# Halved first loads, an earlier weight split and 256-column Fourier products in a token-mixing kernel

## The chip, the cores and the metric

The kernel runs on one core of a Trainium2 chip. The time is the device time of one execution in microseconds; the median of three runs is 1002.89 us (1002.65 to 1003.63). The engines are named as in the profile: PE multiplies matrices, PEld loads its weights, DVE and ACT are the vector and the scalar engine, POOL is little used here, and SP issues the DMAs.

## What is computed

One layer of a diffusion backbone over 1024 latent tokens and 256 context tokens of width 1024, in float32. Cut to what matters:

```python
x = x + sincos_2d(n_lat, D)                              # position
h = rms_norm(x, norm_g) * (1 + sc) + sh                  # sc, sh, gt from silu(c) @ ada_w + ada_b
u_lru, z_lru, u_fft, z_fft, u_pool, z_pool, gates = split(h @ w_in)   # 56 blocks of 128 columns
ya = (bidirectional RG-LRU(conv(u_lru)) * silu(z_lru)) @ proj_a
yb = (fourier_mix(u_fft) * silu(z_fft)) @ proj_b         # fft2 over tokens and channels, 4 groups of 128
yc = (pool_mix(u_pool) * silu(z_pool)) @ proj_c
m = sigmoid(g0) * ya + sigmoid(g1) * yb + sigmoid(g2) * yc
out = rms_norm(x + gt * (m @ w_out)) * final_g
```

## The kernel before

Everything lies transposed, channels on the 128 partitions and tokens along the free axis. A float32 product is made of three products of float32r parts: each operand is split into a high part (ACT casts it) and a low part (DVE subtracts it), and high x low, low x high and high x high are added up in PSUM. So each weight and each activation costs a cast on ACT and a subtraction on DVE before PE can use it.

**The first 120 us** are written out in program order for all engines. The eight `z` blocks of 128 output columns (the gate of the LRU branch) are computed first, and the first six of them before the norm is known: `xs` is x times the weights' scale `gsc`, without the norm's factor `rstd` (`xs_hi`, `xs_lo`, L337 to L342), and `rstd` is multiplied in afterwards. `wave(k, ...)` (L355) does the products of one 128-channel slice k for a set of blocks: three terms, each over the blocks and both 512-token halves, 24 products of 512 columns for the four blocks z0 to z3 (`FIRST`). Their weights come in four chunks of two k each (`load_chunk`, L273), z4 to z7 as whole blocks. For each k DVE does a dot product of `ada` and `silu(c)` for `gsc` (`dot_scale`), adds the position (`add_pos`), makes the low part of xs and adds up the squares (`squares_add`, L422). Before the waves PE runs sixteen dummy products (`warm_up(16)`, L398), each of which the profile shows as two records.

Wave 7 goes block by block: z2, z0, z1, then the sum over the partitions of the squares (`ss`, a product with ones), then z3; ACT copies z2, z0 and z1 out (`copy_out`, L403) and computes `rstd` by Ln and Exp (`rstd_part`). Then blocks z4 and z5 (`NEXT`) run over all k. In the order of ACT the split of z5's weights (L473) stands behind the norm and behind the third `copy_out`. Blocks z6 and z7 (`LAST`) use the normed `ht`, which DVE and ACT make meanwhile.

**The rest** is a list of units (L1111 to L1114) in which PE's order is fixed: 46 more blocks of `w_in` with the LRU's work between them, pooling (`m`), the projections `c` (pooling) and `b` (Fourier) of 24 products each, and the Fourier steps S1 (`s`) and S2 (`t`) in the order `c0 c1 s0 c2 s1 t0 c3 s2 t1 c4 s3 t2 c5 t3`. There the order of the other engines and the buffers of the pools come from a planner that simulates the program; buffers are `p4` (36 of 4 KB a partition), `p2`, and `pacc` (four PSUM tiles of two banks).

S1 of a group (L931) multiplies the folded tokens, nine blocks of 128 (eight and one extra for the middle row), by the channel transform of the group: cosine for blocks 0 to 3 and the extra one, sine for 4 to 7. Each block takes three products of 128 columns. `group_dft` (L906) makes those transforms, high and low, in four separate p2 tiles. The result is split again for S2. `load_fold` (L921) fetches and splits the tokens of a group beforehand.

Of the kernel before, what the change touches and what calls it, by code (L numbers as in the profile page):

```python
# [15 lines left out]
NK = 8  # L16
HALF = 512
# [11 lines left out]
def tile_hybrid_mixer(  # L29
# [106 lines left out]
    class Weight:  # L136
        def __init__(self, name, src, shape=(128, NK, 128), pools=(praw, pwt, pwt)):
            self.name, self.shape, self.pools = name, shape, pools
            self.raw = f4(name + "_f", shape, pools[0])
            SP.dma_start(out=self.raw, in_=src)  # L140

        def mk(self):
            self.hi, self.lo = (r4(self.name + n, self.shape, p) for n, p in zip(("_h", "_l"), self.pools[1:]))
# [98 lines left out]
    with tc.manual_schedule(engines={ET.PE}):  # L242
# [22 lines left out]
        def load_ada(n):  # L265
            ada_t[n] = f4(f"ada{n}")
            SP.dma_start(out=ada_t[n], in_=ada[n])
# [11 lines left out]
        def load_w(nm):  # L279
            wt[nm] = Weight("w" + nm, item(nm)[1], KK, (praw, p4, p4))  # L280

        SP.dma_start(out=sb[0], in_=cc[0:1, :].to_broadcast([128, 1024]))
        load_ada(8)
        for k in range(NK):
            SP.dma_start(out=xt[k], in_=xT[k])
            if k == 0:
                SP.dma_start(out=pos, in_=k_pos)
                SP.dma_start(out=sml, in_=small)
            else:
                load_ada(8 + k)  # L290
            if k in (0, 2, 4):
                load_chunk(k // 2)
        SP.dma_start(out=edge, in_=k_edge)

# [59 lines left out]

        def wave(k, ws, src):  # L355
            for n in range(3):
                for nm, hi, lo in ws:
                    o = pacc_t[nm]
                    for h in range(2):
                        x = src[k][n == 2][:, H[h]]  # L360
                        PE.matmul(out=bank(o, h), lhsT=lo if n == 1 else hi, rhs=x,  # L361
                                  start=k == 0 and n == 0, stop=k == NK - 1 and n == 2)

        def chunk(k, names):
            w = chunks[k // 2]
# [29 lines left out]

        act(sb[0], sb[0], AF.Silu)
        V.tensor_scalar(b1, sml[:, O_AB + 8:O_AB + 16], 1.0, 0.0, op0=ALU.add, op1=ALU.add)
        warm_up(16)  # L398
        sqs, zv = None, {}
        pacc_t = {"z0": acc("z0"), "z1": acc("z1"), "z2": acc("z2"), "z3": acc("z3")}  # L400

# [23 lines left out]
                del sq[k]  # L425


        add_pos(0)
        for k in range(NK):
            dot_scale(k, 0)  # L430
            if k == 0:
                chunks[0].ready()
            xs_hi(k)
            sq[k] = f4(f"sq{k}")
            act(sq[k], xt[k], AF.Square)
            if k < NK - 1:
                add_pos(k + 1)
            if k:
                squares_add(k - 1)
            xs_lo(k)  # L440
            if k % 2 and k < NK - 1:
                chunks[k // 2 + 1].ready()
            if k == 0:
                load_chunk(3)
            if k == 3:
                load_w("z4")
            if k == 4:
                load_w("z5")
            if 1 < k < 6:
                load_ada(k - 2)  # L450
            if k < NK - 1:
                wave(k, chunk(k, FIRST), xs)
        act(rss[:, 0:1], eps, AF.Ln)
        wt["z4"].ready()
        wave(7, chunk(7, ["z2"]), xs)
        copy_out("z2")
        wave(7, chunk(7, ["z0"]), xs)
        wave(7, chunk(7, ["z1"]), xs)
        ps = acc("ss")
        ps = [ps[:, sl] for sl in H]  # L460
        squares_add(7)
        for h in range(2):
            PE.matmul(out=ps[h], lhsT=ones, rhs=sq[0][:, H[h]], start=True, stop=True)
        sq.clear()
        copy_out("z0")
        rstd_part([rstd[:, H[0]], rstd[:, H[1]]], ps)
        copy_out("z1")
        wave(7, chunk(7, ["z3"]), xs)
        dot_shift(0, 0)
        load_ada(4)  # L470
        dot_shift(1, 0)
        load_ada(5)
        wt["z5"].ready()  # L473
        dot_shift(2, 0)
        load_ada(6)
        dot_shift(3, 0)
# [429 lines left out]

        def group_dft():
            cg, fw = pq["cg"], pq["fw"]
            pq["h"], pq["l"] = [], []
            ps = acc("pq")  # L910
            for n in range(2):
                PE.matmul(out=ps[:, H[n]], lhsT=cg[:, n * 128:(n + 1) * 128], rhs=fw, start=True, stop=True)
            for n in range(2):
                hi, lo = r2(f"pqh{n}"), r2(f"pql{n}")
                split(hi, lo, ps[:, H[n]])
                pq["h"].append(hi)
                pq["l"].append(lo)

        ff = {}

# [9 lines left out]

        def S1(g):  # L931
            fh, fl, ex = ff.pop(("f", g))
            o, o2 = acc(f"s1_{g}"), acc(f"s1e_{g}")
            for b in range(8):
                n = b // 4
                ph, pl = pq["h"][n][:, g * 128:(g + 1) * 128], pq["l"][n][:, g * 128:(g + 1) * 128]
                sl = slice(b * 128, (b + 1) * 128)
                mm3(o[:, sl], [(fh[:, sl], fl[:, sl], ph, pl)])
            mm3(o2[:, 0:128], [(ex[:, 0, :], ex[:, 1, :], pq["h"][0][:, g * 128:(g + 1) * 128],
                                pq["l"][0][:, g * 128:(g + 1) * 128])])  # L940
            ah, al = r4(f"ah{g}"), r4(f"al{g}")
            split(ah, al, o)
            xe = p1.tile([128, 2, 128], F32R, tag="t1", name=f"xe{g}")
            split(xe[:, 0, :], xe[:, 1, :], o2[:, 0:128])
            ff["a", g] = (ah, al, xe)

        ysb, ysc = [None] * 4, [None] * 4
# [436 lines left out]
```

## Time and profile before

| | |
|---|---|
| median of 3 runs | 1002.89 us (1002.65 to 1003.63) |
| the profiled execution | 1002.09 us, of which its span (first to last instruction) 1000.3 us |
| PE busy | 988.7 us (99%), 4686 products |
| weight loads (PEld) | 810.3 us (81%) |
| DVE, ACT, POOL busy | 582.1 (58%), 522.2 (52%), 21.7 us (2%) |
| DMA | 152.53 MB, 43% of 16 engines |
| mean granted clock of PE | 0.997 |

Each line of a timeline has the start and the length of an instruction, or of several alike (x8), in microseconds, then engine, line, operation and `output<-inputs`; in brackets the idle time of the engine before it and what ended it. Successive products overlap in the array, so the distance between two starts is what a product costs, not its length. The chain that ended last is 94% PE, 4% ACT and 1% DMA.

### The profile page before, as it was taken

To read this page: it belongs to the slowest core of one execution; us is meant where nothing else is said; L and a number is where in the kernel's file an instruction comes from. 1 tells how busy PE (TensorE), PEld (TensorE's weight loads), DVE (VectorE), ACT (ScalarE), POOL (GpSimd) and SP (SyncE) were. 2 spreads that over 40 slices of the span, in tenths; PEclk is the share of its full clock that TensorE was granted. 3 is DMA by queue.
4 is the path that set the end of the run, shared out by engine and by line. 5 is a ranking of instruction groups with operands and counts; after the bars stand their busy time and mean duration, and the time that the engine had idled before them with its cause. 6 is when DMAs were issued, how large, how long until landed. Compare 5 with 4: busy or idle time off the path is not lost.

```text
span 1000.3 us, 11785 instructions
## 1 busy us (share of the span) xinstructions
PE 988.7 (99%) x4686; PEld 810.3 (81%) x4686; DVE 582.1 (58%) x746; ACT 522.2 (52%) x618; POOL 21.7 (2%) x22
## 2 busy tenths in 40 slices
PE   9989999999999999999999999999999999999997
PEld 5868788878788887888878888778888888888886
DVE  6959457538557485563845628256565674456063
ACT  4443464295793956939599394884332221213131
POOL 0000000000000000000000000000000000000341
PEclk9999999999999999999999999999999999999999
DMA  9532595131322222343243312357655785324272
GB/s 347 229 108 83 197 382 231 64 105 67 108 103 96 101 85 90 127 166 134 70 167 105 132 64 95 106 184 258 217 185 187 244 315 188 137 91 134 71 252 75
DMA packets 48838, 152.53 MB, mean 152 GB/s; under 512 B 6544, under 2 KB 10128, under 8 KB 48784
## 3 DMA queue, kind: packets, MB, share of 16 engines
q1 hardware_dynamic: 48640, 151.53, 43.0%
q8 instruction: 37, 0.61, 0.2%
q10 hardware_dynamic: 144, 0.26, 0.1%
q14 instruction: 17, 0.14, 0.0%
HBM read 114.01 MB, written 37.75 MB: 152 GB/s over the span
## 4 chain that ended last, share of the span: by engine, by line
PE 94%; ACT 4%; DMA 1%; DVE 0%; issue 0%; POOL 0%; DVEq 0%; SPq 0%; POOLq 0%
PE z L361 9%; PE pi L193 3%; PE pg L193 3%; PE o L195 3%; PE pi L195 3%; PE o L193 3%; PE o L194 3%; PE pi L194 3%; PE pg L194 3%; PE ppa L195 3%; PE ppa L193 3%; PE pu L195 3%; PE pg L195 3%; PE pu L194 3%; PE pu L193 3%; PE ppa L194 3%
## 5 line engine op out<-in xcount | busy, mean ns | idle before, releaser
L114 ACT ACT_TABLE_LOAD x74 | 94.9, 1283 | 2.0 <-PEq L1374 0.7
L117 DVE TENSOR_TENSOR i<-i,xc 128x1024 f32<-128x1024 f32 x16 | 19.0, 1223 | 58.9 <-ACT i L114 58.9
L194 PE MATMUL o<-wo_l,mh 128*128 128x512 f32 (+1 forms) x136 | 51.2, 377 | 0.0
L195 PE MATMUL o<-wo_h,mh 128*128 128x512 f32 (+1 forms) x136 | 51.2, 376 | 0.0
L193 PE MATMUL o<-wo_h,ml 128*128 128x512 f32 (+1 forms) x136 | 51.2, 376 | 0.0
L193 PE MATMUL pi<-hh,i_l 128*128 128x512 f32 x128 | 50.8, 397 | 0.0
L193 PE MATMUL ph<-hh,h_l 128*128 128x512 f32 x128 | 50.5, 395 | 0.2
L193 PE MATMUL pg<-hh,g_l 128*128 128x512 f32 x128 | 50.5, 394 | 0.0
L194 PE MATMUL pi<-hl,i_h 128*128 128x512 f32 x128 | 49.9, 390 | 0.0
L195 PE MATMUL ph<-hh,h_h 128*128 128x512 f32 x128 | 49.9, 390 | 0.0
L195 PE MATMUL pi<-hh,i_h 128*128 128x512 f32 x128 | 49.9, 390 | 0.0
L194 PE MATMUL ph<-hl,h_h 128*128 128x512 f32 x128 | 49.8, 389 | 0.0
L194 PE MATMUL pg<-hl,g_h 128*128 128x512 f32 x128 | 49.8, 389 | 0.0
L195 PE MATMUL pg<-hh,g_h 128*128 128x512 f32 x128 | 49.8, 389 | 0.0
L193 PE MATMUL pu<-hh,u_l 128*128 128x512 f32 x128 | 49.8, 389 | 0.0
L194 PE MATMUL pu<-hl,u_h 128*128 128x512 f32 x128 | 49.8, 389 | 0.0
L195 PE MATMUL pu<-hh,u_h 128*128 128x512 f32 x128 | 49.8, 389 | 0.0
L193 PE MATMUL ppa<-yh,pa_l 128*128 128x512 f32 x128 | 49.8, 389 | 0.0
L194 PE MATMUL ppa<-yl,pa_h 128*128 128x512 f32 x128 | 49.8, 389 | 0.0
L195 PE MATMUL ppa<-yh,pa_h 128*128 128x512 f32 x128 | 49.8, 389 | 0.0
L129 ACT CAST xh<-xc 128x1024 fp32r<-128x1024 f32 x8 | 8.4, 1054 | 75.1 <-DVE xc L120 52.8
L120 DVE SCALAR_TENSOR_TENSOR junk<-ada,sb 128x1024 bf16<-128x1024 f32 x32 | 39.0, 1219 | 13.5 <-DMA ada<-in_ada 13.5
(378 smaller groups left out, 2614.8 us busy)
## 6 DMA issues: line engine op xcount, KB each, us to landing
ada<-in_ada SPq DMA_DIRECT2D x32, 512.0 KB, 8.6
x<-in_xT SPq DMA_DIRECT2D x8, 512.0 KB, 10.0
u_f<-in_w_in SPq DMA_DIRECT2D x8, 512.0 KB, 4.0
i_f<-in_w_in SPq DMA_DIRECT2D x8, 512.0 KB, 4.5
k_i<-ei SPq DMA_DIRECT2D x8, 512.0 KB, 2.9
z<-k_z SPq DMA_DIRECT2D x8, 512.0 KB, 5.4
k_y<-z SPq DMA_DIRECT2D x8, 512.0 KB, 2.6
h_f<-in_w_in SPq DMA_DIRECT2D x8, 512.0 KB, 4.3
```

Source lines behind the costliest of these rows:

```text
L114: S.activation(out=o, in_=i, func=func, **kw)
L117: V.tensor_tensor(o, a, b, op=op)
L120: V.scalar_tensor_tensor(o, a, s, b, op0=op0, op1=op1, **kw)
L129: S.copy(hi, src)
L193: PE.matmul(out=o, lhsT=wl, rhs=xh, start=first and i == 0, stop=False)
L194: PE.matmul(out=o, lhsT=wh, rhs=xl, start=False, stop=False)
L195: PE.matmul(out=o, lhsT=wh, rhs=xh, start=False, stop=last and i == n - 1)
L361: PE.matmul(out=bank(o, h), lhsT=lo if n == 1 else hi, rhs=x, start=k == 0 and n == 0, stop=k == NK - 1 and n == 2)
```

## The change

- **First loads.** `small` goes ahead of `ada8` and x0. x0 and the first weight chunk come in two halves each (x by tokens, weights by k); for the other k, `ada` is loaded ahead of x. `first_block` does the first two k's weights and the first x: ACT casts the weights of k = 0, then the two halves of x as DVE adds their positions, then the weights of k = 1; DVE makes the low parts. In wave 0 the first term runs over the first token half of all four blocks before the second half.
- **Dummies.** Seven instead of sixteen.
- **Norm.** `squares_add(7)` is issued ahead of wave 7, `copy_out("z0")`, two shift dots and the split of z5's weights ahead of the wave of z1, `copy_out("z1")` ahead of the sum of squares.
- **Fourier step.** High and low transform lie beside each other in one p4 tile, so that the high part of a token block is multiplied by both in one product of 256 columns, which go to two column ranges of PSUM; the low part is multiplied by the high transform (128 columns). This holds for seven of the eight blocks; block 7 and the extra one keep three products of 128 columns. ACT copies one column range to SBUF (`v`) and DVE adds the other; the split for S2 reads `v`. PSUM tiles stay two a group.

```diff
@@ -137,7 +137,8 @@
         def __init__(self, name, src, shape=(128, NK, 128), pools=(praw, pwt, pwt)):
             self.name, self.shape, self.pools = name, shape, pools
             self.raw = f4(name + "_f", shape, pools[0])
-            SP.dma_start(out=self.raw, in_=src)
+            if src is not None:
+                SP.dma_start(out=self.raw, in_=src)
 
         def mk(self):
             self.hi, self.lo = (r4(self.name + n, self.shape, p) for n, p in zip(("_h", "_l"), self.pools[1:]))
@@ -279,16 +280,21 @@
         def load_w(nm):
             wt[nm] = Weight("w" + nm, item(nm)[1], KK, (praw, p4, p4))
 
+
         SP.dma_start(out=sb[0], in_=cc[0:1, :].to_broadcast([128, 1024]))
+        SP.dma_start(out=sml, in_=small)
         load_ada(8)
-        for k in range(NK):
+        SP.dma_start(out=pos, in_=k_pos)
+        w0 = Weight("wc0", None, (128, 4, 2, 128), CHUNK_POOLS[0])
+        for h in range(2):
+            SP.dma_start(out=xt[0][:, H[h]], in_=xT[0][:, H[h]])
+            SP.dma_start(out=w0.raw[:, :, h, :],
+                         in_=w_in[B_ZLRU:B_ZLRU + 4, :, h, :].rearrange("b p o -> p b o"))
+        chunks.append(w0)
+        for k in range(1, NK):
+            load_ada(8 + k)
             SP.dma_start(out=xt[k], in_=xT[k])
-            if k == 0:
-                SP.dma_start(out=pos, in_=k_pos)
-                SP.dma_start(out=sml, in_=small)
-            else:
-                load_ada(8 + k)
-            if k in (0, 2, 4):
+            if k in (2, 4):
                 load_chunk(k // 2)
         SP.dma_start(out=edge, in_=k_edge)
 
@@ -354,12 +360,13 @@
 
         def wave(k, ws, src):
             for n in range(3):
-                for nm, hi, lo in ws:
-                    o = pacc_t[nm]
-                    for h in range(2):
-                        x = src[k][n == 2][:, H[h]]
-                        PE.matmul(out=bank(o, h), lhsT=lo if n == 1 else hi, rhs=x,
-                                  start=k == 0 and n == 0, stop=k == NK - 1 and n == 2)
+                order = [(w, h) for w in ws for h in range(2)]
+                if k == 0 and n == 0:
+                    order.sort(key=lambda v: v[1])
+                for (nm, hi, lo), h in order:
+                    x = src[k][n == 2][:, H[h]]
+                    PE.matmul(out=bank(pacc_t[nm], h), lhsT=lo if n == 1 else hi, rhs=x,
+                              start=k == 0 and n == 0, stop=k == NK - 1 and n == 2)
 
         def chunk(k, names):
             w = chunks[k // 2]
@@ -395,7 +402,7 @@
 
         act(sb[0], sb[0], AF.Silu)
         V.tensor_scalar(b1, sml[:, O_AB + 8:O_AB + 16], 1.0, 0.0, op0=ALU.add, op1=ALU.add)
-        warm_up(16)
+        warm_up(7)
         sqs, zv = None, {}
         pacc_t = {"z0": acc("z0"), "z1": acc("z1"), "z2": acc("z2"), "z3": acc("z3")}
 
@@ -425,19 +432,37 @@
                 del sq[k]
 
 
-        add_pos(0)
+        def first_block():
+            w = chunks[0]
+            w.mk()
+            dot_scale(0, 0)
+            x, e = xt[0].rearrange("p (r c) -> p r c", c=64), pos[:, 0:16].unsqueeze(2).to_broadcast([128, 16, 64])
+            xs[0] = r4("xh0"), r4("xl0")
+            S.copy(w.hi[:, :, 0, :], w.raw[:, :, 0, :])
+            for h in range(2):
+                r = slice(8 * h, 8 * h + 8)
+                tt(x[:, r], x[:, r], e[:, r], ALU.add)
+                act(xs[0][0][:, H[h]], xt[0][:, H[h]], scale=gsc[0][0])
+            S.copy(w.hi[:, :, 1, :], w.raw[:, :, 1, :])
+            for r in range(2):
+                tt(w.lo[:, :, r, :], w.raw[:, :, r, :], f(w.hi[:, :, r, :]), ALU.subtract)
+                if not r:
+                    xs_lo(0)
+            w.raw = None
+
+        first_block()
         for k in range(NK):
-            dot_scale(k, 0)
-            if k == 0:
-                chunks[0].ready()
-            xs_hi(k)
+            if k:
+                dot_scale(k, 0)
+                xs_hi(k)
             sq[k] = f4(f"sq{k}")
             act(sq[k], xt[k], AF.Square)
             if k < NK - 1:
                 add_pos(k + 1)
             if k:
                 squares_add(k - 1)
-            xs_lo(k)
+            if k:
+                xs_lo(k)
             if k % 2 and k < NK - 1:
                 chunks[k // 2 + 1].ready()
             if k == 0:
@@ -452,25 +477,25 @@
                 wave(k, chunk(k, FIRST), xs)
         act(rss[:, 0:1], eps, AF.Ln)
         wt["z4"].ready()
+        squares_add(7)
         wave(7, chunk(7, ["z2"]), xs)
         copy_out("z2")
         wave(7, chunk(7, ["z0"]), xs)
+        copy_out("z0")
+        for k in range(2):
+            dot_shift(k, 0)
+        wt["z5"].ready()
         wave(7, chunk(7, ["z1"]), xs)
+        copy_out("z1")
         ps = acc("ss")
         ps = [ps[:, sl] for sl in H]
-        squares_add(7)
         for h in range(2):
             PE.matmul(out=ps[h], lhsT=ones, rhs=sq[0][:, H[h]], start=True, stop=True)
         sq.clear()
-        copy_out("z0")
         rstd_part([rstd[:, H[0]], rstd[:, H[1]]], ps)
-        copy_out("z1")
         wave(7, chunk(7, ["z3"]), xs)
-        dot_shift(0, 0)
         load_ada(4)
-        dot_shift(1, 0)
         load_ada(5)
-        wt["z5"].ready()
         dot_shift(2, 0)
         load_ada(6)
         dot_shift(3, 0)
@@ -906,15 +931,13 @@
 
         def group_dft():
             cg, fw = pq["cg"], pq["fw"]
-            pq["h"], pq["l"] = [], []
             ps = acc("pq")
             for n in range(2):
                 PE.matmul(out=ps[:, H[n]], lhsT=cg[:, n * 128:(n + 1) * 128], rhs=fw, start=True, stop=True)
+
             for n in range(2):
-                hi, lo = r2(f"pqh{n}"), r2(f"pql{n}")
-                split(hi, lo, ps[:, H[n]])
-                pq["h"].append(hi)
-                pq["l"].append(lo)
+                pq[n] = r4(f"pq{n}", (128, 4, 2, 128))
+                split(pq[n][:, :, 0, :], pq[n][:, :, 1, :], ps[:, H[n]].rearrange("p (g o) -> p g o", g=4))
 
         ff = {}
 
@@ -930,18 +953,29 @@
 
         def S1(g):
             fh, fl, ex = ff.pop(("f", g))
-            o, o2 = acc(f"s1_{g}"), acc(f"s1e_{g}")
-            for b in range(8):
-                n = b // 4
-                ph, pl = pq["h"][n][:, g * 128:(g + 1) * 128], pq["l"][n][:, g * 128:(g + 1) * 128]
-                sl = slice(b * 128, (b + 1) * 128)
-                mm3(o[:, sl], [(fh[:, sl], fl[:, sl], ph, pl)])
-            mm3(o2[:, 0:128], [(ex[:, 0, :], ex[:, 1, :], pq["h"][0][:, g * 128:(g + 1) * 128],
-                                pq["l"][0][:, g * 128:(g + 1) * 128])])
-            ah, al = r4(f"ah{g}"), r4(f"al{g}")
-            split(ah, al, o)
+            v, ah, al = f4(f"s1{g}"), r4(f"ah{g}"), r4(f"al{g}")
             xe = p1.tile([128, 2, 128], F32R, tag="t1", name=f"xe{g}")
-            split(xe[:, 0, :], xe[:, 1, :], o2[:, 0:128])
+            q = [pq[n][:, g, :, :] for n in range(2)]
+
+
+            for n, m in enumerate((4, 3)):
+                o = acc(f"s1_{g}_{n}")
+                for b in range(m):
+                    sl = slice((4 * n + b) * 128, (4 * n + b + 1) * 128)
+                    d = o[:, b * 256:(b + 1) * 256]
+                    PE.matmul(out=d, lhsT=fh[:, sl], rhs=q[n], start=True, stop=False)
+                    PE.matmul(out=d[:, 0:128], lhsT=fl[:, sl], rhs=q[n][:, 0, :], start=False, stop=True)
+                if n:
+                    sl = slice(896, 1024)
+                    mm3(o[:, 768:896], [(fh[:, sl], fl[:, sl], q[1][:, 0, :], q[1][:, 1, :])])
+                    mm3(o[:, 896:1024], [(ex[:, 0, :], ex[:, 1, :], q[0][:, 0, :], q[0][:, 1, :])])
+                w = o[:, 0:256 * m].rearrange("p (b e c) -> p b e c", e=2, c=128)
+                vn = v[:, n * HALF:n * HALF + 128 * m].rearrange("p (b c) -> p b c", c=128)
+                S.copy(vn, w[:, :, 1, :])
+                tt(vn, vn, w[:, :, 0, :], ALU.add)
+            S.copy(v[:, 896:1024], o[:, 768:896])
+            split(xe[:, 0, :], xe[:, 1, :], o[:, 896:1024])
+            split(ah, al, v)
             ff["a", g] = (ah, al, xe)
 
         ysb, ysc = [None] * 4, [None] * 4
```

## Rows read from the trace of the kernel before

**Rows 1.** The waits of PE: who was waited for, us in total, times, longest.

```profile
PE z L361 <- ACT wz_h L129: 3.9, 1, 3.9
```

**Rows 2.** Busy time after that wait: stretch, length, engines busy (instructions), granted clock, DMA.

```profile
66.72:70.52 3.80, 3.80 (x10) 3.05 (x11) 3.73 (x8) 0.00 (x0) 0.00 (x0) 0.60 0.11 26
```

**Rows 3.** Timeline, the start: dummies' weights, DVE's first instruction, first xh, first product.

```profile
8.34 0.19 PEld L310 LDWEIGHTS warm<-warm 128*128 128x128 f32 x1 [0.24 <-issue]
...
8.78 0.17 DVE L397 TENSOR_SCALAR sc<-sml 128x8 f32<-128x8 f32 x1 [7.92 <-DMA sml<-in_small]
...
11.53 1.15 ACT L114 ACTIVATE xh<-x,gsc 128x1024 fp32r<-128x1024 f32 x1 [0.22 <-DVE gsc L120]
...
16.52 2.41 PE L361 MATMUL z<-xh,wc_h 128*128 128x512 f32 x8
```

**Rows 4.** Timeline: dot 1 and xh1, xh6, waves 6 and 7, wz4, last squares.

```profile
14.88 1.22 DVE L120 SCALAR_TENSOR_TENSOR junk<-ada,sb 128x1024 bf16<-128x1024 f32 x1
...
16.39 1.15 ACT L114 ACTIVATE xh<-x,gsc 128x1024 fp32r<-128x1024 f32 x1 [2.77 <-DVE gsc L120]
...
43.91 1.15 ACT L114 ACTIVATE xh<-x,gsc 128x1024 fp32r<-128x1024 f32 x1 [3.01 <-issue]
...
49.59 1.98 PE L361 MATMUL z<-xh,wc_h 128*128 128x512 f32 x8
...
52.24 1.04 ACT L129 CAST wz_h<-wz_f 128x1024 fp32r<-128x1024 f32 x1
...
54.45 1.22 DVE L117 TENSOR_TENSOR sq<-sq,sq 128x1024 f32<-128x1024 f32 x1
...
55.03 0.62 PE L361 MATMUL z<-xh,wc_h 128*128 128x512 f32 x2
```

**Rows 5.** First chunk's cast; issue of ada9, and its us to landing (last column).

```profile
10.27 1.04 ACT L129 CAST wc_h<-wc_f 128x1024 fp32r<-128x1024 f32 x1 [3.85 <-DMA wc_f<-in_w_in]
...
4.51 0.52 SPq L267 DMA_DIRECT2D ada<-in_ada  x1
...
ada<-in_ada SPq DMA_DIRECT2D x1, 512.0 KB, 8.3
```

**Rows 6.** Timeline: sum of squares, z3 scaled, z7's low weight, its block's second term.

```profile
59.12 1.88 PE L463 MATMUL ss<-sq,ones 128*128 128x512 f32 x4
...
70.81 1.28 DVE L117 TENSOR_TENSOR vz<-z,rstd 128x512 f32<-128x512 f32 x2
...
87.09 1.22 DVE L134 TENSOR_TENSOR wz_l<-wz_f,wz_h 128x1024 fp32r<-128x1024 f32 x1
...
90.49 1.07 PE L361 MATMUL z<-hh,wz_l 128*128 128x512 f32 x4
```

**Rows 7.** Timeline of PE: two neighbours in S1 (128 columns) and in S2 (256).

```profile
718.37 0.27 PE L194 MATMUL s<-pql,fh 128*128 128x128 f32 x1
718.48 0.28 PE L195 MATMUL s<-pqh,fh 128*128 128x128 f32 x1
...
731.30 0.28 PE L193 MATMUL sv<-th,al 128*128 128x256 f32 x1
731.42 0.28 PE L194 MATMUL sv<-tl,ah 128*128 128x256 f32 x1
```

**Rows 8.** Timeline: copies out, fold load, its low part, PE's wait, third S1.

```profile
56.59 1.08 ACT L407 COPY vz<-z 128x512 f32<-128x512 f32 x2 [3.31 <-PE z L361]
...
721.42 1.61 SPq L107 DMA_DIRECT2D fo<-k_UF  x1
...
730.81 1.23 DVE L134 TENSOR_TENSOR fl<-fo,fh 128x1024 fp32r<-128x1024 f32 x1 [1.12 <-ACT fh L129]
...
733.23 0.50 PE L193 MATMUL p<-c0h,pc_l 128*128 128x512 f32 x1 [0.33 <-DVE al L134]
...
738.82 0.22 PE L193 MATMUL s<-pqh,fl 128*128 128x128 f32 x1
```

## Prediction

> **What bounds the kernel.** I read the page's busy shares first, then PE's waits, then the timeline of the few stretches that the change touches. PE is busy for 98.9% of the span, and of its listed waits only two lie inside the kernel: 3.9 us for wz_h, the split weight of the sixth block [rows 1], and 0.3 us for al in the Fourier stage [rows 8]. The first costs more than its length: after it the granted clock is 0.60 over 3.80 us, in which ten products run [rows 2]. At full clock they would take 3.80 x 0.60 = 2.28 us, so the wait costs 3.87 + 1.52 = 5.4 us. A third loss is no wait in the list: PE multiplies a dummy until 16.52 us, while the first xh is done at 11.53 + 1.15 = 12.68 us [rows 3]. Everywhere else a saving has to come out of PE's own products.
>
> The second bound is DVE's pace in the first 55 us. One k of the four-block wave takes PE 55.03 - 49.59 = 5.44 us, and DVE needs nearly as long for its dot, position add, squares add and low part, so an earlier PE runs into DVE. How far ahead PE can go is read from the xh rows [rows 4].
>
> **The start.** Seven dummies instead of sixteen are 14 records instead of 32. The weights of the 14th are loaded at 8.34 us and one record takes 0.43 us there (records 14 to 32 fill 8.34 to 16.52), so PE is free at about 9.0 us [rows 3]. What it waits for then is data. Before the first chunk, the same bytes are queued as now, except that small goes ahead of ada8 and x0 and the weights come in halves. The first chunk lands at 10.27 us, 1.49 us after small (8.78), in pieces of 1 KB; x1 and ada9, 4 KB a row, land after it at 1.27 us each, ada9 at 4.51 + 8.3 = 12.8 us [rows 3, 5]. The halves have pieces of 512 B (weights) and 2 KB (x). The step from 4 KB to 1 KB cost 0.22 us per 512 KB; 512 B adds twice as many pieces again, so I take 0.3 to 0.4 us more for the two weight halves together, and as ends nothing and a full doubling (1.5 us). So the first halves are there at about 8.2 (x) and 9.1 us (weights), DVE's half add and ACT's two half casts (0.54 us each by the copies of 128x512 [rows 8]) follow, and PE starts at about 10.3 us. The gap without a product is then 1.3 us; no row before shows what the clock does after one so long. If it falls, 3.8 us at 0.60 lose 1.5 us of a wave that has 1.3 us to spare, as the next point shows, so 0.2 us at most; staying up costs nothing, which I take.
>
> The Trainium skill ("DMA: Bandwidth & Descriptors", Specifications) says that pieces from 512 B up run at line rate. By it the halves would cost nothing and the sum below would be 0.4 us better; the 1 KB pieces of this trace, 1.49 against 1.27 us, already do not agree.
>
> The second wave is what counts. DVE's order is now dot 0, two half adds, low weights, low x, low weights, position add 1, dot 1. x1 is now behind ada9 and lands where ada9 does today, later by the halves' 0.4 us: 13.2 us. DVE is free before (half adds done by 10.4, then 0.6 + 1.2 + 0.6 us of low parts to 12.9). Position add 1 ends at 14.4 (1.22 us as for the other 128x1024 adds), dot 1 takes 1.51 us until xh1 starts (14.88 to 16.39), so xh1 starts at 15.9 instead of 16.39 us: DVE's whole chain is 0.5 us earlier, no more, since nothing else of it changes before k = 7 [rows 4]. Wave 0 from 10.3 us ends at 15.7; wave 1 waits for xh1 until 17.05. From there PE follows DVE. The latest of the xh rows against 5.44 us a wave is xh6: done at 45.06 us now, 44.6 then, so wave 7 starts at 44.6 + 5.44 = 50.0 instead of 55.03 us [rows 4].
>
> **The norm.** Three blocks of wave 7 take 18 x 0.2267 = 4.1 us, to 54.1. The sum of squares needs squares_add(7), which ends at 54.45 + 1.22 = 55.67 us now and 55.2 then, so it is the next thing that is late, by 1.1 us. It starts at 55.2 instead of 59.12 us: 3.9 us gained [rows 4, 6]. The fourth block follows as before. The fifth and sixth then run without the wait, if wz5's split is done. On ACT it moves from behind both norm steps and the third evacuation to behind the second one: wz4's cast (52.24 us today, so 51.7 to 52.8 [rows 4]), then two evacuations of 1.08 us [rows 8] and a cast of 1.05 end at 56.0, before the 58.3 us at which PE gets there. On DVE two shift dots (2.7 us) stand ahead of it: 55.2 + 2.7 + 1.2 = 59.1, and PE wants the low part 1.36 us into the blocks, at 59.7. The cover is 0.6 us; if it is gone by 1 us, that is the cost. Behind these ACT instructions the Ln and Exp of the norm wait, about 1 us longer behind the sum than now; that is off PE's path, since 21.8 us of blocks five and six lie in front of the first product that needs rstd. The stall's 5.4 us go whole. Start and norm together: 3.9 + 5.4 = 9.3 us. Ends: 7 (DVE's chain late by the 1.5 us of slow pieces, plus the lost cover) and 10.5 us (no cost of halves).
>
> Whether blocks seven and eight keep that lead is DVE's affair again. It scales z3 at 70.81 us now; then it is free after two more dots at about 62, a lead of 8.8 us against PE's 9.3. The tightest operand after it is z7's low weight, done at 87.09 + 1.22 = 88.3 us for a product at 90.49 + 0.45: 2.6 us of slack for 0.5 us [rows 6]. The loads of the moved steps (ada 2 to 7, z6, z7) stand in SP's queue behind DVE's dots, as now, and move with them. In all that follows PE has the one wait of 0.3 us, and what feeds it there hangs on PE's and DVE's own progress, so the lead is carried to the end.
>
> **The Fourier step.** Today a group takes 27 products of 128 columns, which follow each other after 0.111 us (718.37 to 718.48); products of 256 columns follow after 0.120 us (731.30 to 731.42) [rows 7]. A 128-column product thus costs almost as much as a 256-column one. After the change a group has seven pairs (256 + 128 columns) and six of 128: 7 x (0.120 + 0.111) + 6 x 0.111 = 2.28 us against 27 x 0.111 = 3.00, so 0.72 us less, 2.9 for four groups. Bounds of a mixed pair, which no row shows: 0.240 (two at the slower spacing), which saves 2.6 us, and 0.222 (two at the faster), which saves 3.1. The added evacuation is per group two strided copies and a short one on ACT (128x512 takes 0.54 us, so 0.54 + 0.41 + 0.27, about 1.2) and as much on DVE; the split then reads SBUF. It stands beside the projection of 24 products, 5.4 us, that lies between S1 and any S2, and ACT and DVE have room. The price is a longer hold on a PSUM tile: the only wait of the stage is one of those today (0.33 us for al, which frees the tile [rows 8]). I take 0.1 us more: 2.8 us. group_dft's splits write other strides for the same count, ahead of their use by 35 us: nothing.
>
> The Trainium skill ("TensorE: Matmul & The Clock Gate", Back-to-back issue gap) gives about 81 ns for a sustained 128-column product with its load and 109 ns for 256 columns. By it a group falls from 2.19 to 1.82 us and the step saves 1.5 us, so 1.3 less than here; the rows, 111 and 120 ns, do not agree with it.
>
> **Sum.** The profiled execution took 1002.09 us (span 1000.3); less 9.3 and 2.8 that is 990.0. The median of the runs is 0.8 us above it, as much as the runs scatter, so I leave the forecast at 990.0 us.
>
> **Rivals.**
> - The start gives less (15%): slow small pieces, the clock, or DVE, whose pace sets the waves. For: the xh rows leave PE no way around DVE. Against: the bytes ahead of x1 are those ahead of ada9 today. With 1.5 us of slow pieces and 1 us of lost cover: 992 to 992.5.
> - The Fourier step gives half or nothing (16%): pairs that cost more than both spacings, or an S1 that waits. v and pq take up to three more of the 36 p4 buffers, and loads there may have to wait for buffers. A fold load takes from its issue at 721.42 to the end of fl at 732.04, 10.6 us [rows 8]. If the third S1 gets its load only after the S2 ahead of it (its end is 733.23 - 0.33 = 732.9), the low part is there at 743.5 and S1, due at 738.8, waits 4.7 us, with the clock's 1.5 us 6.2: 996.2. Without a wait but with half the saving: 991.4. The rule of the Trainium skill on the issue gap, above, ends there too.
> - Slower (3%): the same mechanism in each of three groups. The second S1 has only one projection of 5.4 us between itself and the first, so it would wait 10.6 - 5.4 = 5.2 us, the others 4.7; with 1.5 us of clock each that is 19.1 us, more than the 12.1 gained: 1009.1. It decides from the point where all three wait; two (12.4 to 12.9 us) make it even. Against it: today none of the three waits reaches PE.
> - More than forecast (6%): no cost of the halves, and the strided reads of x in halves let DVE start earlier: 988 to 988.5.
>
> **How the numbers follow.** The forecast with its bounds (7 to 10.5 and 2.6 to 3.1 us) has 60% and its own range is 988.4 to 992.4. Below it 6%, above it 34%: 15 at about 992, 16 between 991.4 and 996.2, 3 for even or slower. The range of 8 in 10 is 987.5 to 995. A change of 0.2% is 2 us, from there on a measurement of this kernel can tell it. Faster than that in all cases but the one with three (or two) waits: 0.95; the same 0.02; slower 0.03.
>
> **What would show it.** Right: the first z product at 10 to 11 us; a wait of about 1 us for xh1; wave 7 at about 50 us; the sum of squares at 55 us after a wait for sq; no wait for wz_h and full clock through 60 to 70 us; the first ZP product about 9.3 us earlier than today; an S1 of 2.3 us. Wrong: a fall of the clock behind the dummies that moves xh1's wave, a wait for wz_l in blocks five to eight, a wait for fl or a PSUM tile between 705 and 765 us, or xh1 later than 16.4 us.

## Result and the profile after

The changed kernel takes 991.25 us (median of 4 runs, 990.68 to 991.89) against 1002.77 us (4 runs, 1002.47 to 1003.63): ratio 0.9884, 95% interval 0.9867 to 0.9901. That is 11.5 us less. The forecast was 990.0 us, its range 987.5 to 995.0. On the chip of the last comparisons the same kernel took 991.70 us.

The profiled execution of after took 990.68 us, span 988.9. TensorE (PE) is busy 977.8 us (99%), VectorE (DVE) 586.8, ScalarE (ACT) 526.9. PE's waits (in all, times, longest):

```profile
PE p L194 <- DVE s L117: 1.4, 1, 1.4
PE warm L316 <- POOL warm L258: 1.3, 1, 1.3
PE z L368 <- ACT xh L114: 1.3, 2, 0.9
PE ss L493 <- DVE sq L117: 0.8, 1, 0.8
```

The wait of 3.9 us of [rows 1] is gone; the forecast short waits for xh and sq came, and one of 1.4 us in the Fourier stage that was not forecast. Behind the norm the granted clock, 0.60 in [rows 2], is now (windows, PE alone: busy, clock, DMA share, GB/s):

```profile
60.00:64.00 4.00, 4.00 (x19) 1.00 0.74 228
64.00:68.00 4.00, 4.00 (x20) 1.00 1.02 402
```

Timeline of after, the lines that answer to [rows 3, 4 and 6]:

```profile
10.10 2.12 PE L368 MATMUL z<-xh,wc_h 128*128 128x512 f32 x8 [0.32 <-ACT xh L114]
...
15.59 1.15 ACT L114 ACTIVATE xh<-x,gsc 128x1024 fp32r<-128x1024 f32 x1 [3.16 <-DVE gsc L120]
...
16.80 2.11 PE L368 MATMUL z<-xh,wc_h 128*128 128x512 f32 x8 [0.94 <-ACT xh L114]
...
49.91 0.61 PE L368 MATMUL z<-xh,wc_h 128*128 128x512 f32 x2
...
54.27 1.07 ACT L129 CAST wz_h<-wz_f 128x1024 fp32r<-128x1024 f32 x1
...
55.00 1.96 PE L493 MATMUL ss<-sq,ones 128*128 128x512 f32 x4 [0.85 <-DVE sq L117]
...
61.56 0.68 DVE L117 TENSOR_TENSOR vz<-z,rstd 128x512 f32<-128x512 f32 x1
...
108.94 0.50 PE L194 MATMUL pZP<-hh,ZP_l 128*128 128x512 f32 x1
```

The first real product comes at 10.10 us instead of 16.52, wave 7 at 49.91 instead of 55.03, the sum of squares at 55.00 instead of 59.12. The first product of ZP, the first block of the list of units, stood at 118.58 us before, so start and norm give 9.64 us in this execution. In the first Fourier step (S1) a pair of products, 256 + 128 columns, follows the last one after 0.24 us (0.23 in the next ones), and the group ends 2.23 us after its start:

```profile
708.33 0.28 PE L966 MATMUL s<-pq,fh 128*128 128x256 f32 x1
...
708.50 0.34 PE L966 MATMUL s<-pq,fh 128*128 128x256 f32 x1
708.68 0.22 PE L967 MATMUL s<-pq,fl 128*128 128x128 f32 x1
708.74 0.34 PE L966 MATMUL s<-pq,fh 128*128 128x256 f32 x1
...
710.56 0.45 PE L194 MATMUL p<-c0h,pc_l 128*128 128x512 f32 x1
```

### The profile page after: what moved, and what is told of

It is laid out like the page before. It is cut to its first block, busy times and chain, and to the rows that moved or that the text cites. A ratio compares the mean times of both kernels' runs of the same rounds, so it can differ in the third digit from the quotient of the medians.

```text
span 988.9 us, 11733 instructions
## 1 busy us (share of the span) xinstructions
PE 977.8 (99%) x4640; PEld 802.7 (81%) x4640; DVE 586.8 (59%) x756; ACT 526.9 (53%) x632; POOL 21.6 (2%) x22
## 4 chain that ended last, share of the span: by engine, by line
PE 90%; ACT 4%; DVE 2%; issue 0%; DVEq 0%
PE z L368 5%; PE pi L194 3%; PE pg L194 3%; PE p L194 3%; PE o L196 3%; PE o L194 3%; PE pi L195 3%; PE pi L196 3%; PE p L195 3%; PE pg L196 3%; PE ppa L194 3%; PE pu L196 3%; PE pg L195 3%; PE o L195 3%; PE pu L195 3%; PE ppa L196 3%
## 5 line engine op out<-in xcount | busy, mean ns | idle before, releaser
L195 PE MATMUL pi<-hl,i_h 128*128 128x512 f32 x128 | 49.9, 390 | 0.0
L196 PE MATMUL ph<-hh,h_h 128*128 128x512 f32 x128 | 49.9, 390 | 0.0
L196 PE MATMUL pi<-hh,i_h 128*128 128x512 f32 x128 | 49.9, 390 | 0.0
```

The lines of the kernel that those rows point to most:

```text
L195: PE.matmul(out=o, lhsT=wh, rhs=xl, start=False, stop=False)
L196: PE.matmul(out=o, lhsT=wh, rhs=xh, start=False, stop=last and i == n - 1)
```

## The experiments

Medians; "before" is the kernel before in the same comparison. The last two columns are worked out from the profiled execution: the start of the first ZP product (start and norm lie before it), and the span less the start of S1's first product (Fourier and output).

| kernel | us | before | ratio, 95% | ZP starts | S1 to end |
|---|---|---|---|---|---|
| before (profiled) | 1002.09 | | | 118.58 | 282.32 |
| after | 991.25 | 1002.77 | 0.9867 to 0.9901 | 108.94 | 280.57 |
| after, again | 991.70 | 1003.07 | 0.9876 to 0.9903 | 109.91 | 280.49 |
| Fourier only | 1002.20 | 1002.48 | 0.9987 to 1.0004 | 119.73 | 281.17 |
| start and norm only | 992.93 | 1002.48 | 0.9886 to 0.9917 | 109.89 | 281.88 |
| whole loads | 991.91 | 1002.48 | 0.9879 to 0.9906 | 110.33 | 280.34 |
| norm as before | 997.78 | 1002.48 | 0.9940 to 0.9965 | 115.58 | 280.60 |
| no dummies | 991.73 | 1002.92 | 0.9875 to 0.9906 | 109.97 | 280.91 |
| 12 dummies in the wait | 1006.98 | 1002.92 | 1.0030 to 1.0055 | 124.03 | 281.73 |
| the same and Fourier | 1005.17 | 1002.92 | 1.0015 to 1.0035 | 124.39 | 280.37 |
| 4 dummies in the wait | 1001.97 | 1003.07 | 0.9980 to 0.9998 | 118.23 | 282.93 |
| fold split later | 989.98 | 1003.07 | 0.9858 to 0.9885 | 109.82 | 278.88 |
| fold split later, squares first | 989.02 | 1003.07 | 0.9847 to 0.9878 | 108.96 | 278.90 |
| seven dummies only | 999.24 | 1002.93 | 0.9950 to 0.9977 | 117.16 | 281.71 |

**Fourier only, and all but Fourier.** The kernel before with after's group_dft and S1; and after with those of before.

> The kernel before with only the new first Fourier step (256-column products for seven of eight blocks). Theory (from the trace of after): each of the four groups falls from 3.00 to 2.28 us, 4 x 0.72 = 2.9 us, and 1.1 us of it is given back by one longer wait, that of the second step's first product of batch 2 (p <- s, DVE), about 1.4 us in place of 0.33. Net -1.8 us: about 1001.0 us. Rival A: the four groups give all of 2.9 us and the longer wait belongs to the other edits: about 999.9 us, with that wait at 0.3 us. Rival B: the longer products gain nothing outside the one profiled run: about 1002.8 us.

> The changed kernel with the first Fourier step of before (128-column products). Theory: all 9.65 us that the trace of after leads by when the Fourier transform starts comes from the start and the norm, so 1002.8 - 9.65 = about 993.1 us, with the wait p <- s back at 0.33 us. Rival: part of the lead is lost again behind the first Fourier step whatever its products are (a wait of 1.4 us stays), about 994.2 us.

All but Fourier came out as expected, 992.93 us, though the wait of 0.33 us that was to come back did not: its trace has neither wait. The Fourier edit alone missed: 0.3 us less, interval from 1.3 less to 0.4 more. Its trace has two waits for s (timeline):

```profile
733.05 0.50 PE L193 MATMUL p<-c0h,pc_l 128*128 128x512 f32 x1 [0.52 <-DVE s L117]
...
745.69 0.50 PE L193 MATMUL p<-c0h,pc_l 128*128 128x512 f32 x1 [1.40 <-DVE s L117]
```

So the stretch from S1 on is 1.15 us shorter than before, not 1.8. The rest went where the edit does not reach. Behind the norm's wait this execution's clock stayed at half longer than in [rows 2] (windows, PE: busy, clock, DMA share, GB/s):

```profile
66.00:68.00 2.00, 1.59 (x4) 0.50 0.00 0
68.00:70.00 2.00, 2.00 (x7) 0.50 0.15 25
70.00:72.00 2.00, 2.00 (x6) 0.50 0.94 297
72.00:74.00 2.00, 2.00 (x9) 0.87 1.03 414
```

**Dummies in the wait.** If the clock behind the wait is what differs, filling the wait should remove it.

```diff
         act(rss[:, 0:1], eps, AF.Ln)
         ...
+        for _ in range(12):      # second kernel: with Fourier; third: range(4)
+            PE.matmul(out=pacc_t["z4"][:, 0:512], lhsT=warm[:, 0:128], rhs=warm, start=True, stop=True)
```

> The kernel before with twelve dummy products (128 x 512, 0.23 us each, 2.7 us in all) put into the wait of 3.9 us ahead of the first products of the sixth and seventh blocks. They change nothing that is computed and end before the wait does. Theory: the wait costs its length and, on top, a stretch of half clock behind it that differs between executions (1.5 us in the profile of before, about 3.3 us in that of the Fourier edit alone); kept busy, TensorE stays at full clock and the time falls by 1.5 to 3 us, to about 1000.5 us, with less spread between runs. Rival: the clock falls whatever is done there, or the dummies push back what follows: 1002.5 us or more.

> The kernel before with the same twelve dummy products and the new first Fourier step. The Fourier edit alone gave only 0.3 us. Theory: its gain was there (two longer waits for the evacuation, 1.9 us in all in place of 0.3, leave 1.3 us of 2.9) and was covered by a longer stretch of half clock behind the wait in the norm; with the clock held up in both kernels this one is 1.3 to 1.8 us under the one with dummies alone, about 999.0 us. Rival: the Fourier edit really gives nothing unless the start is changed: the two kernels with dummies are within 0.5 us of each other.

Twelve was my error of size: a dummy is a plain float32 product, two records that start 0.43 us apart, so twelve fill 10.5 us:

```profile
62.95 10.46 PE L484 MATMUL z<-warm 128*128 128x512 f32 x24
```

The Trainium skill ("FP8 and Floating Point Precision", TensorE Precision Notes) says that true FP32 takes 4 passes; the trace agrees roughly: 0.86 us for a dummy is 3.8 times the 0.228 us of a 512-column product of the waves.

The overfilled wait makes both kernels slower, so both expected times, 1000.5 and 999.0 us, missed; but the clock reads 1.00 behind it in both and the pair answers its question: with Fourier 1005.17, without 1006.98, 1.8 us less, of which the profiled executions show 1.4 from S1 on. The edit's gain does not depend on the start.

> The kernel before with four dummy products in the wait of 3.9 us, in place of twelve, which overfilled it: a dummy is two passes of 0.436 us, not 0.23 us, so that twelve took 10.5 us. Four take 3.5 us and end with the wait. Theory: the clock then stays at 1.00 behind the wait, and the 1.5 to 3 us that the half clock costs come off: 1000 to 1001.3 us. Rival: the clock's fall is not caused by the idle time: 1002.5 us or more.

With four, the clock stays up (windows of PE, as above):

```profile
66.00:68.00 2.00, 1.57 (x6) 1.00 0.00 0
68.00:70.00 2.00, 1.94 (x9) 1.00 0.00 0
```

and over all runs the mean granted clock is 0.9994, against 0.9970 in the kernel before. The kernel gains 1.1 us (0.2 to 2.0), less than the 1.8 to 3.1 that the theory gave: in the profiled execution 0.6 us is lost again from S1 on, where PE waits 1.0 us for al in place of 0.33. The price of the clock can be read between two fixed groups of products, one ahead of the wait and the third xh row behind it. Timelines of four dummies, of before, and of Fourier only:

```profile
61.16 1.03 PE L361 MATMUL z<-xh,wc_h 128*128 128x512 f32 x2
...
67.44 0.73 PE L361 MATMUL z<-xh,wz_h 128*128 128x512 f32 x2 [0.43 <-ACT wz_h L129]
...
70.20 1.07 PE L361 MATMUL z<-xh,wz_h 128*128 128x512 f32 x4
...
72.92 1.07 PE L361 MATMUL z<-xh,wz_h 128*128 128x512 f32 x4
```

```profile
60.43 1.03 PE L361 MATMUL z<-xh,wc_h 128*128 128x512 f32 x2
...
73.27 1.07 PE L361 MATMUL z<-xh,wz_h 128*128 128x512 f32 x4
```

```profile
60.13 1.03 PE L361 MATMUL z<-xh,wc_h 128*128 128x512 f32 x2
...
74.41 1.08 PE L361 MATMUL z<-xh,wz_h 128*128 128x512 f32 x4
```

That is 11.76, 12.84 and 14.28 us, so the half clock cost 1.1 us in one execution and 2.5 in the other: the 1.4 us more that the Fourier kernel paid there hid its 1.15 in these two executions. For the medians this is not shown: over all runs the mean granted clock is the same with and without the Fourier edit (0.9972 in 11 runs, 0.9969 in 15), and the interval does not exclude a gain of 1.15 us. The prediction's 1.5 us was the lost clock alone. With four dummies, too, ten products take 2.76 us from 67.44 to 70.20, 0.5 more than at 0.228 us each: the weight loads wait for wz_l, which VectorE splits from 67.42 to 68.65 (timeline of PEld, four dummies):

```profile
68.70 0.30 PEld L361 LDWEIGHTS z<-xh,wz_l 128*128 128x128 f32 x2 [0.50 <-DVE wz_l L134]
```

The spread between runs does not follow this wait: it is 3.0 us in the kernel before (1001.3 to 1004.2), which has the wait, and 3.0 us with four dummies, where the clock stays up; it is 1.2 us in norm as before and in seven dummies only, which have the wait and fewer runs. What makes it stays open.

**The start.** Whole loads: the loads and the first block of before, with seven dummies and the new norm and Fourier code. No dummies: after without warm_up(7). Seven dummies only: the kernel before with one number changed.

```diff
-        warm_up(16)
+        warm_up(7)
```

> The changed kernel with whole loads of x and of the weights in the order of before and the first block's code of before, but seven dummy products instead of sixteen; the norm and Fourier edits stay. Theory: VectorE's pace sets the first waves: the first product starts 2.6 us later (about 12.7 us) but the second wave still waits for the second scaled x, which comes at about 16.4 + 1.15 us instead of 15.6 + 1.15, so only 0.8 us are lost: about 992.05 us. Rival: TensorE's own start decides, the 2.6 us are lost in full: about 993.9 us.

> The changed kernel without its seven dummy products at the start. Theory: the first products then run at half of the clock, but the second wave waits for the second scaled x anyway until 16.8 us and the waits of TensorE in the first two waves are about as long as what the clock costs, so 0 to +0.3 us: 991.25 to 991.6 us, with the granted clock under 1 in the first waves and the seventh wave still at 49.9 us. Rival: the clock's price comes on top, +1.5 to +1.8 us, about 993 us, with the seventh wave about 1.7 us later.

> The kernel before with seven dummy products at the start in place of sixteen, and nothing else. Theory: nearly all that the start gives comes from this: with whole loads and the edits to norm and Fourier the sum of squares started at 56.4 us instead of 59.12, so 2.7 us here, about 1000.1 us, with the first product at about 12.5 us behind an idle time of 2.8 us and the wait of 3.9 us in the norm unchanged. Rival A: without the halves the idle time ahead of the first product lowers the clock and VectorE holds the second wave, so that under 1 us is left: about 1002 us. Rival B: all nine dummies that go come off, 4.1 us: about 998.7 us.

The halves hardly matter: without them the kernel is 0.2 to 0.7 us slower (against the two medians of after, taken in other comparisons), though its first product comes at 12.53 us and not at 10.10. The theory's time came, 991.91 for 992.05 us, but not by its path. The second wave does not wait for xh1, which is done at 17.35 us (timeline of whole loads):

```profile
12.53 3.68 PE L364 MATMUL z<-xh,wc_h 128*128 128x512 f32 x8 [2.77 <-ACT xh L114]
...
19.72 1.98 PE L364 MATMUL z<-xh,wc_h 128*128 128x512 f32 x8
```

From its first product to the sum of squares at 56.45 us PE has no wait in the list. In after and its repeat it has two, 0.94 us for xh1 and 0.85 to 0.89 for sq. A later start, at half clock (0.51 from 14 to 16 us), eats these waits up, and only the rest reaches the sum of squares: 0.5 us against the repeat (55.99). Nor do the seven dummies matter: without them 991.73 us, the same as after again. The second wave starts without a wait there too (18.90 us), wave 7 comes at 51.54 us, 0.67 later than in the repeat and not at the 49.9 expected, and the wait for sq shrinks from 0.89 to 0.25 us. Nearly all that the start gives is the sixteen dummies that were in the way. One number gives 3.7 us (2.3 to 5.0), more than expected and less than rival B, which the interval does not exclude. The profiled execution has half clock behind an idle time of 3.4 us, as rival A had it (its time, 1002 us, did not come), and its sum of squares at 57.34 us, not 56.4 (timeline of seven dummies only, then a window with all engines):

```profile
12.48 3.78 PE L361 MATMUL z<-xh,wc_h 128*128 128x512 f32 x8 [3.38 <-ACT xh L114]
```

```profile
11.10:14.70 3.60, 2.22 (x5) 1.82 (x6) 3.60 (x5) 2.10 (x2) 0.00 (x0) 0.51 1.02 395
```

This execution, the slowest of the five (1000.07 us), is 2.0 us under the profiled one of before: 1.4 up to ZP, and 0.6 from S1 on, where the old wait of 0.33 us is missing. The other 1.7 us of the 3.7 are the distances of the two medians from their profiled executions, 0.8 us each; what makes these was not measured.

**Norm as before.** wz5's split, squares_add(7) and the evacuations in the old order; the rest as after.

```diff
         wave(7, chunk(7, ["z0"]), xs)
-        copy_out("z0")
-        for k in range(2):
-            dot_shift(k, 0)
-        wt["z5"].ready()
         wave(7, chunk(7, ["z1"]), xs)
         ...
+        dot_shift(1, 0)
+        wt["z5"].ready()
```

> The changed kernel with the order of before around the norm (the sixth block's weights are split behind the norm's statistics again); start and Fourier edits stay. Theory: the wait of 3.9 us for the sixth block's high weight part comes back, and with it the stretch of granted clock at 0.60 that cost 1.5 us: +5.4 us, about 996.65 us, and the wait and a granted clock under 1 are seen in the profile. Rival: only the wait returns, the clock stays at 1.0: about 995.1 us.

Wait and half clock are back (timeline, windows of PE), and the kernel loses 6.1 to 6.5 us against the two medians of after (expected 5.4):

```profile
63.29 1.45 PE L368 MATMUL z<-xh,wz_h 128*128 128x512 f32 x3 [4.10 <-ACT wz_h L129]
```

```profile
62.00:64.00 2.00, 0.71 (x2) 0.89 0.00 0
64.00:66.00 2.00, 2.00 (x6) 0.50 0.03 8
66.00:68.00 2.00, 2.00 (x9) 0.76 0.58 184
```

4.10 us, and 0.71 x 0.11 + 2 x 0.50 + 2 x 0.24 = 1.6 us of clock. From the first product to ZP it is 115.58 - 10.67 = 104.91 against 98.84 us in after: 6.07, so 0.4 us is not named. The old place of squares_add(7) costs nothing here: the wait for sq is 0.85 us, as in after.

**The new wait in Fourier.** In after, PE stands for 1.4 us until 734.12. It needs the PSUM tile of the third S1, whose first and last products start at 727.04 and 729.16 us. VectorE and ScalarE empty it late, because the split of the next folded matrix (ex, fh, fl) stands ahead (PE, DVE, then ACT):

```profile
727.04 0.28 PE L966 MATMUL s<-pq,fh 128*128 128x256 f32 x1
...
734.12 0.50 PE L194 MATMUL p<-c0h,pc_l 128*128 128x512 f32 x1 [1.40 <-DVE s L117]
```

```profile
729.52 1.22 DVE L134 TENSOR_TENSOR b0l<-yb,b0h 128x1024 fp32r<-128x1024 f32 x1
730.65 0.15 DVE L133 CAST ex<-fo 128x1 fp32r<-128x1 f32 x1
...
732.24 1.23 DVE L134 TENSOR_TENSOR fl<-fo,fh 128x1024 fp32r<-128x1024 f32 x1 [1.11 <-ACT fh L129]
733.38 1.14 DVE L117 TENSOR_TENSOR s<-s,s 128x512 f32<-128x512 f32 x2
```

```profile
731.16 1.05 ACT L129 CAST fh<-fo 128x1024 fp32r<-128x1024 f32 x1 [2.37 <-DVE fo L950]
732.11 0.96 ACT L974 COPY s<-s 128x512 f32<-128x512 f32 x2
```

Two edits move what is late behind what is awaited: the fold's split to two units before its S1, and squares_add(7) ahead of wz4's split.

```diff
         def load_fold(g):
             ...
+            ff["w", g] = (w, fh, fl, ex)
+
+        def split_fold(g):
+            w, fh, fl, ex = ff.pop(("w", g))
             split(ex[:, 0, 0:1], ex[:, 1, 0:1], w[:, 512:513], "dve")
             ...
+            on(pos_of[f"s{n}"] - 2, split_fold, n)
```

```diff
-        wt["z4"].ready()
         squares_add(7)
+        wt["z4"].ready()
```

> The changed kernel once more, as the base for the two below on the same chip: 991.25 us as measured, within 0.5 us; the landings of the first loads differ by up to 1 us between the profiles so far (first product at 10.10, 10.67, 11.02 us).

> The changed kernel with the split of the folded Fourier matrices emitted two units later, so that VectorE evacuates the first step's third group before it splits the matrices of the fourth. Theory: the new wait of 1.4 us (p <- s) comes from that order on VectorE, since the tile that it waits for is complete 5 us before; it falls to about 0.3 us and the kernel is 1.1 us faster than the changed kernel, about 990.15 us. Rival: the evacuation is late for another reason (ScalarE's copy, or the matrices' load), the wait stays or goes to the first step's last group: 991.25 us.

> The changed kernel with the later split of the folded matrices and with the last sum of squares on VectorE ahead of the split of the fifth block's weights. Theory: besides the 1.1 us above, the wait of 0.85 us of the sum of squares goes, in all 1.9 us: about 989.3 us. Rival: VectorE's later low weight part of the fifth block is now waited for by the first products of that block in the norm's shadow, or the statistics had slack: no gain beside the other edit, 990.15 us.

The evacuation now comes first on DVE and the split of the low part behind it (timeline, fold split later):

```profile
731.54 1.15 DVE L117 TENSOR_TENSOR s<-s,s 128x512 f32<-128x512 f32 x2
732.60 0.15 DVE L133 CAST ex<-fo 128x1 fp32r<-128x1 f32 x1
...
735.28 1.22 DVE L134 TENSOR_TENSOR fl<-fo,fh 128x1024 fp32r<-128x1024 f32 x1
```

PE has no wait there, and the kernel is 1.7 us under after again (expected 1.1). But the split stood ahead in the kernel before, too: fl ends at 732.04 us there, and al right behind it is what PE waited 0.33 us for, [rows 8] and here:

```profile
726.48 0.22 PE L193 MATMUL s<-pqh,fl 128*128 128x128 f32 x1
...
731.96 1.22 DVE L134 TENSOR_TENSOR al<-s,ah 128x1024 fp32r<-128x1024 f32 x1
```

Counted from the start of the third S1, PE could use the tile after 733.23 - 0.33 - 726.48 = 6.42 us before and gets it after 6.75; in after these are 5.68 and 7.08. So of the 1.07 us that the wait grew by, 0.33 is a later evacuation, and 0.74 is PE's own saving, for which it comes earlier to a tile that is not free.

With both edits the kernel takes 989.02 us, 2.7 us under after again and 14 under before, and the sum of squares starts at 55.08 us without a wait, although the first product came as late as 11.11 us. It is the fastest version of this study.

## Why the prediction was right, and the term that was not

- **Start, 3.9 us to the sum of squares.** Right: 59.12 to 55.00 in the two profiled executions, with wave 7 at 49.91 (forecast 50.0), the wait for xh1 (0.94, forecast about 1) and for sq (0.85, forecast 1.1). The repeat lies 1 us later from the first landing on (first product 11.08, xh1 at 16.57, sum of squares 55.99): the forecast fell between two executions. The sum of squares of before is no fixed mark either: 58.81 to 60.20 us in the five traces with sixteen dummies at the start. That the time of the first product counts for little is shown by whole loads and no dummies. That VectorE's pace holds PE is seen in the two waits of after; without halves or dummies PE does not wait for xh1, and the sum of squares comes 0.46 and 0.04 us later than in the repeat. The cause that the prediction weighed most, the halves, is nearly without effect in either direction.
- **The norm, 5.4 us.** Right in mechanism, a little small: 6.1 to 6.5 us come back with the old order. The low part of wz5 is done at 57.45 + 1.23 = 58.68 us, before PE needs it at about 59.5; the cover, forecast at 0.6 us, was 0.9. z3 is scaled at 61.56, a lead of 9.25 us, not 8.8, so the lead reached the end whole. The clock's 1.5 us is no fixed price: 1.1 and 2.5 us in two executions. Norm as before takes back three edits at once; the wait for wz_h with its half clock is 5.7 of the 6.07 us there.
- **The Fourier products, 2.9 us.** Right. S1 to the end is 281.7 to 281.9 us in the three kernels with the old step and no wait there, 278.9 in the two with the new step and no wait (278.88 and 278.90): 2.9 us. The pair costs 0.23 us, the sum of the two spacings in [rows 7]. The 1.5 us that the prediction sets beside this mixes two figures of the Trainium skill ("TensorE: Matmul & The Clock Gate", Back-to-back issue gap): 81 ns is a sustained gap, 109 ns for 256 columns an isolated one. The prediction's sum does not use them.
- **"The price is a longer hold on a PSUM tile ... I take 0.1 us more".** This is the term that failed. The new step with its wait ends 280.3 to 280.9 us after S1's start (281.2 with the two waits of Fourier only), 1.4 to 2.0 us later than without; the old wait of 0.33 us was worth 0.5. I added up the evacuation's own 1.2 us and found room beside the projection, but did not write down what stands ahead of it on VectorE and ScalarE at that time. The fold's split stood there already, and PE already waited behind it, as [rows 8] show. So the longer hold was the smaller part (0.33 of 1.07 us); the larger is that a PE which finishes the third S1 0.74 us sooner only comes sooner to the same queue. The rival on folds asked if the load is late, and it was not; its split came too early.

By what was measured, the first S1 starts 717.98 - 708.33 = 9.65 us earlier and the rest is 282.32 - 280.57 = 1.75 us shorter: 1002.09 - 9.65 - 1.75 = 990.69, the profiled execution's own time. Against the forecast's 9.3 and 2.8 us the start and norm gave 0.35 more and the Fourier stage 1.05 less, so part of the nearness is two errors of opposite sign. The prediction saw the median of before 0.8 us above its profiled execution and left that out. The two medians of after lie 0.6 and 1.0 us above it; the repeat's profiled execution, 991.64 us, differs by the first landing, 0.97 us at the first ZP product. Two small figures of the prediction are a tenth off: PE's share is 988.7 of 1000.3 us, 98.8%, and its bounds give 988.5 to 992.5 us.

## What to carry to other kernels

When a step gets shorter or its evacuation changes, list everything queued ahead of what frees its tile, on each engine that takes part, not only the evacuation's own duration: here a split due much later stood in front, and the wait behind it grew by 1.07 us, about two thirds of it time that the matrix engine had just saved; taking the split away gave 1.7 us. A wait of the matrix engine can cost more than its length: behind 3.9 us of it the half clock cost 1.1 and 2.5 us in two executions, while behind the 1.4 us of the Fourier wait in after the clock reads 1.00. And before loads are cut finer, take away what was put in to fill the time: one number gave a third of the gain, the halves 0.2 to 0.7 us.

## What was not expected of the hardware

Without dummies the first eight products start 0.45 us apart (3.58 us from the first to the ninth), about twice their later 0.228, while the window of 11.10 to 14.70 us reads a granted clock of 1.00 (all engines, no dummies):

```profile
11.10:14.70 3.60, 3.58 (x8) 2.82 (x9) 3.38 (x5) 2.19 (x3) 0.00 (x0) 1.00 1.01 403
```

With both edits the same products take 3.65 us behind 2.09 us of idle time, and there the column reads 0.53. Without dummies PE had not worked before; with both edits the seven dummies had run. So at an engine's first work in an execution the column does not show the slow pace; the products' spacing does. The sixteen dummies at the start show it as well. With records 0.43 us apart, the last one 0.59 us long, all 32 would take 13.9 us; in the five traces that have them they take 15.45, 15.77, 16.50, 16.50 and 16.84 us, the first ones slowly (four records from 2.20 to 4.40 us in each, six or seven in a stretch of that length from 11.00 us on), and the column reads 1.00 all along. The longest, of Fourier with twelve dummies:

```profile
1.31 16.84 PE L310 MATMUL warm<-warm 128*128 128x512 f32 x32 [1.31 <-POOL warm L257]
```

The Trainium skill ("TensorE: Matmul & The Clock Gate", Part 1: The HAM clock gate) says that the number of slow products at the start differs between runs of one kernel; these five traces, of kernels with the same start, agree.

Behind 1.79 us of idle time (start and norm only) and 1.33 (after again) they took 2.14 and 2.12 us. What sets this apart from 2.09 us was not tried.
